# Two ring sizes in one weight stream: raw buffers from three to four, split buffers from six to five

## The chip, the cores and the metric

The kernel runs on one core of a Trainium2 chip. The metric is device time in microseconds of one execution. An execution was timed three times; the trace comes from one further, profiled execution. The engines of the core are named as the profile names them: PE is the matrix engine (TensorE), with PEld for its weight loads; DVE, ACT and POOL are the vector, scalar and GpSimd engines; SP is the engine that issues the weight loads.

## The reference, cut to what matters

Two transformer blocks run one after the other on 256 tokens of 1024 channels, batch 1, all in float32.

```python
# first block
mod = silu(c) @ ada_w + ada_b                    # six rows of 1024: shifts, scales, gates
u = rms_norm(h, norm1_g) * (1 + scale1) + shift1
z = u @ w_in                                     # q, k, v of two attentions, gates
y_a = nsa_attention(...) @ w_up_nsa              # 8 heads, softmax rows
y_b = stick_breaking_attention(...) @ w_up_sb
h = h + gate1 * ((sigmoid(m_a) * y_a + sigmoid(m_b) * y_b) @ w_out)
u2 = rms_norm(h, norm2_g) * (1 + scale2) + shift2
h = h + gate2 * (square(relu(u2 @ mlp_w1)) @ mlp_w2)
# second block
x = x + 0.5 * swiglu(rmsnorm(x, ffn1_norm), ffn1_w_gu, ffn1_w_down)
z = rmsnorm(x, mix_norm) @ w_in
merged = gate0 * (spatial_gating @ w_branch_a) + gate1 * (mla @ w_branch_b) + gate2 * (memory_attention @ w_branch_c)
x = x + merged @ w_out
x = x + 0.5 * swiglu(rmsnorm(x, ffn2_norm), ffn2_w_gu, ffn2_w_down)
```

The work is a long row of products of 256 tokens with weight matrices, and every weight is used once.

## The kernel before, in words

**The weight stream.** The host lays all weights out in the order of their use. The stream is cut into 191 chunks of up to 128 x 2048 float32 (1 MB), and each chunk into pieces of up to 1024 columns. Class `Stream` (L279) brings them in. `pump` (L303) issues the load of a chunk on SP (L320) into one of `RB` raw ring buffers of 8 KB a partition, once the chunk that had the buffer is used up. Some chunks of the start have buffers of their own and don't count.

**The split.** Each product is computed as three matmuls of numbers rounded to a short float: hi by hi, hi by lo, lo by hi. So each piece is split before use: `_split` (L332) writes hi on ACT (L342, tile wh), and lo, the difference of raw and hi, is written on DVE (L330, tile wl) when the next piece is split or the piece is used. hi and lo go into two pools of `HB` buffers each, of 4 KB a partition. A piece may only be split when fewer than `HB` pieces are split and not yet released (`_can`, L351); a piece is released by `done` behind its last product, and releases count in order.

**Which piece next.** After each product the program calls `fill` (L380), which splits up to three pieces as long as they lie at most four ahead of the one in use and `_can` allows it. So the place of a split in ACT's and DVE's order is set when the program is written: if `_can` says no, it is written after the next release, behind whatever other instructions the program has put on ACT and DVE in between. All engines work their instructions in order.

**What stands in the stream beside the split pieces.** The adaLN weights (labels `ada`) are not split: DVE multiplies them into a sum (L513; in the first normalization `first`, L506 and L509, with POOL taking some, L499). A finished sum is split itself for a column sum on PE: `put` (L356) takes a buffer of the hi and lo pools for it until `drop`. In the MLP this is so for gate2, from step p = 12 of the hidden columns to p = 14, where two copies (L1400) bring the row out.

**Where pieces are held long.** `lin_B` (L618) goes over its four pieces once for each half of the tokens and releases them in the second pass: this is so for the vb pieces of the attention stage and for the four kvm pieces of each half of the memory keys and values. `down_tail` (L1223) does the same with the last four pieces of a feed-forward stage, while it adds residuals (L1196, L1202) and takes squares for the next norm (L579, L581, L585).

**The attention stage.** Beside the products of the weight stream a planner interleaves the attention's own steps by estimated costs. `nsa` (L982) makes for each head a row block: scores on PE, the maximum on DVE (L995), exponentials on ACT (L997), the normalization on DVE (L999, L1000, L1002), then three transposes on PE (L1006) and a copy on ACT (L1008). Up to three heads go as a group; the tiles are ns2, ns3 and so on for the heads.

Of the kernel before, what the change touches and what calls it, by code (L numbers as in the profile page):

```python
# [276 lines left out]


class Stream:  # L279
    RB = 3  # L280
    HB = 6

    def __init__(self, tc, pools, wst, ada):
        self.nc, self.wst, self.ada = tc.nc, wst, ada
# [21 lines left out]
    def pump(self):  # L306
        while self.dma < len(CHUNKS):
# [3 lines left out]
            else:  # L311
                last = self.ring[-self.RB] if len(self.ring) >= self.RB else -1
                if last >= self._chunks_used():
# [37 lines left out]
    def _can(self):  # L351
        if self.at >= len(SUBS) or SUBS[self.at]["chunk"] >= self.dma:
            return False
        return SUBS[self.at]["kind"] == "ada" or self.seq - self.released < self.HB

    def put(self, t):  # L356

        assert self.seq - self.released < self.HB
        hi = self.hi_pool.tile([P, 1024], F32R, tag="whi", name=f"ph{self.seq}")
# [50 lines left out]
def _model(es, tc, nc, x_in, mem_in, wst, sm_in, rows_in, w1_in, cw2_in, sgw_in, posi_in, cst_in, cst1_in, oh_in, out, dbg):  # L410
# [3 lines left out]
    per = es.enter_context(tc.tile_pool(name="per", bufs=1))  # L414
    raw_p = es.enter_context(tc.tile_pool(name="raw", bufs=Stream.RB))
    hi_p = es.enter_context(tc.tile_pool(name="whi", bufs=Stream.HB))
    lo_p = es.enter_context(tc.tile_pool(name="wlo", bufs=Stream.HB))
    xp = es.enter_context(tc.tile_pool(name="xT", bufs=2))
# [1453 lines left out]
```

## Time and profile before

| what | value |
|---|---|
| three timed runs | 1081.32, 1081.81, 1083.03 us |
| median | 1081.81 us |
| profiled execution | 1083.37 us, its span 1081.6 us |
| busy: PE, PEld | 1047.4 us (97%), 946.7 us (88%) |
| busy: DVE, ACT, POOL | 689.3 us (64%), 573.8 us (53%), 77.5 us (7%) |
| weight stream's DMA queue | 198.74 MB, 50.7% of the DMA engines' time |
| 331 splits: hi on ACT, lo on DVE | 1029 ns and 1223 ns each |
| 1 MB load, issue to landing | 5.0 us (median of 170) |

PE is busy nearly all of the span, so idle time of the other engines costs nothing by itself. A row of the timeline gives start, duration, engine, line, operation, the tiles written and read, and in brackets how long the engine was idle before it and what ended the wait. PEclk in a row of windows is the granted clock of PE, 1.00 for the upper of two levels.

### The profile page before, as it was taken

The numbers are of one execution on the slowest core, as the hardware profiler recorded it, in microseconds if no ns is written. First come the engines' busy times: TensorE is split into PE (matmuls) and PEld (weight loads), VectorE is DVE, ScalarE is ACT, GpSimd is POOL, SyncE is SP. The second block draws the span as 40 slices with busy tenths as digits, with TensorE's granted clock in tenths as the row PEclk, the third lists the DMA queues.
The fourth block names the chain that finished last, engine by engine and source line by source line (L and its number), as shares of the span: only waits on it lengthen the run. The fifth ranks groups of instructions, "written<-read, shape, count | busy, mean of one in ns | idle before, by whom it ended". The sixth has DMA issues, their size and how long they took to land.

```text
span 1081.6 us, 16916 instructions
## 1 busy us (share of the span) xinstructions
PE 1047.4 (97%) x6909; PEld 946.7 (88%) x6909; DVE 689.3 (64%) x1058; ACT 573.8 (53%) x938; POOL 77.5 (7%) x85
## 2 busy tenths in 40 slices
PE   4899999999999999999999999999999999999998
PEld 3788678898899998889999998889999989999997
DVE  5976866768777665666545557578554886455543
ACT  5257565465664454555444445667666655444441
POOL 4400011120100010000000000100000500000000
PEclk9889999999999999999999999999999999999999
DMA  8675425755666645465555454744333655554541
GB/s 338 259 287 179 175 85 195 264 192 167 229 233 238 252 172 191 178 206 183 188 202 190 161 195 162 248 163 154 117 108 117 207 212 195 195 195 156 197 182 50
DMA packets 31961, 206.07 MB, mean 191 GB/s; under 512 B 3811, under 2 KB 5132, under 8 KB 9996
## 3 DMA queue, kind: packets, MB, share of 16 engines
q1 hardware_dynamic: 30028, 198.74, 50.7%
q0 software_dynamic: 1856, 6.26, 1.8%
q8 instruction: 54, 0.88, 0.3%
q14 instruction: 23, 0.19, 0.1%
HBM read 203.93 MB, written 1.06 MB: 190 GB/s over the span
## 4 chain that ended last, share of the span: by engine, by line
PE 77%; DVE 2%; ACT 1%; issue 0%; ACTq 0%
PE ps_a L455 39%; PE ps_w L455 36%; PE ps_t L561 1%; PE ps_t L455 1%; DVE wl L330 1%; PE ps_t L1718 0%; PE ps_w L1751 0%; PE ps_t L1790 0%; DVE u_l L611 0%; DVE xr L1196 0%; DVE SG L1195 0%; DVE SG L592 0%; PE ps_t L1574 0%; ACT x_h L602 0%; DVE SG L585 0%
## 5 line engine op out<-in xcount | busy, mean ns | idle before, releaser
L330 DVE TENSOR_TENSOR wl<-raw,wh 128x1024 fp32r<-128x1024 f32 (+2 forms) x331 | 392.6, 1223 | 76.9 <-ACT wh L342 76.4
L342 ACT ACTIVATE wh<-raw 128x1024 fp32r<-128x1024 f32 (+2 forms) x331 | 325.6, 1029 | 19.0 <-DMA raw<-in_wst_dram 9.9
L455 PE MATMUL ps_w<-x_h,wh 128*128 128x256 f32 x640 | 181.2, 283 | 0.0
L455 PE MATMUL ps_w<-x_h,wl 128*128 128x256 f32 x640 | 181.1, 283 | 0.0
L455 PE MATMUL ps_w<-x_l,wh 128*128 128x256 f32 x640 | 181.1, 283 | 0.0
L455 PEld LDWEIGHTS ps_w<-x_l,wh 128*128 128x128 f32 x640 | 122.7, 192 | 1.4
L455 PEld LDWEIGHTS ps_w<-x_h,wh 128*128 128x128 f32 x640 | 122.7, 192 | 1.4
L455 PEld LDWEIGHTS ps_w<-x_h,wl 128*128 128x128 f32 x640 | 122.7, 192 | 0.0
L455 PE MATMUL ps_w<-u_h,wh 128*128 128x256 f32 x224 | 63.4, 283 | 0.0
L455 PE MATMUL ps_w<-u_l,wh 128*128 128x256 f32 x224 | 63.4, 283 | 0.0
L455 PE MATMUL ps_w<-u_h,wl 128*128 128x256 f32 x224 | 63.4, 283 | 0.0
L455 PE MATMUL ps_a<-hmix_h,wh 128*128 128x256 f32 x192 | 57.1, 297 | 0.0
L455 PE MATMUL ps_a<-u_h,wh 128*128 128x256 f32 x192 | 56.5, 294 | 0.0
L455 PE MATMUL ps_a<-hmix_l,wh 128*128 128x256 f32 x192 | 54.3, 283 | 0.0
L455 PE MATMUL ps_a<-hmix_h,wl 128*128 128x256 f32 x192 | 54.2, 282 | 0.0
L455 PE MATMUL ps_a<-u_l,wh 128*128 128x256 f32 x192 | 54.2, 282 | 0.0
L455 PE MATMUL ps_a<-u_h,wl 128*128 128x256 f32 x192 | 54.2, 282 | 0.0
L455 PE MATMUL ps_a<-wh,hh 128*128 128x512 f32 x128 | 50.3, 393 | 0.0
L455 PE MATMUL ps_a<-wl,hh 128*128 128x512 f32 x128 | 50.1, 391 | 0.2 <-DVE wl L330 0.2
L455 PE MATMUL ps_a<-wh,hl 128*128 128x512 f32 x128 | 49.9, 390 | 0.0
L1420 ACT ACTIVATE f2r<-ps_w 128x256 f32<-128x256 f32 x20 | 7.7, 385 | 78.1 <-PE ps_w L455 78.1
L1421 DVE TENSOR_TENSOR f2r<-f2r,ps_w 128x256 f32<-128x256 f32 x20 | 8.4, 421 | 62.1 <-ACT f2r L1420 62.1
(494 smaller groups left out, 2400.7 us busy)
## 6 DMA issues: line engine op xcount, KB each, us to landing
raw<-in_wst_dram SPq DMA_DIRECT2D x170, 1024.0 KB, 5.0
raw<-in_wst_dram SPq DMA_DIRECT2D x9, 768.0 KB, 4.2
raw<-in_wst_dram SPq DMA_DIRECT2D x4, 792.0 KB, 8.2
raw<-in_wst_dram SPq DMA_DIRECT2D x3, 512.0 KB, 10.8
xr<-in_x_dram SPq DMA_DIRECT2D x2, 512.0 KB, 4.8
cw<-in_w_dram POOLq DMA_DIRECT2D x1, 1024.0 KB, 5.1
NB<-Dr SPq DMA_DIRECT2D x1, 1024.0 KB, 10.1
f<-in_rows_dram POOLq DMA_DIRECT2D x2, 512.0 KB, 4.3
```

The lines of the kernel that those rows point to most:

```text
L330: self.nc.vector.tensor_tensor(lo, raw, hi.bitcast(F32), op=OP.subtract)
L342: self.nc.scalar.activation(hi[:, :w], raw, AF.Copy)
L455: PE.matmul(o, l, r, start=start, stop=stop, skip_group_check=True)
L561: PE.transpose(bank[:, j * P:(j + 1) * P], src[:, (f0 + j) * P:(f0 + j + 1) * P], ident)
L1420: ACT.activation(r, b[:, :256], AF.Silu)
L1421: DVE.tensor_tensor(r, r, b[:, 256:512], op=OP.mult)
```

## The change

Two constants of `Stream`: the raw ring has four buffers of 8 KB a partition instead of three, and the hi and the lo pool have five buffers of 4 KB each instead of six. The bytes in SBUF stay the same.

```diff
 class Stream:
-    RB = 3
-    HB = 6
+    RB = 4
+    HB = 5
```

The pools are made with these sizes (`bufs=Stream.RB`, `bufs=Stream.HB`), and `pump`, `_can` and `put` decide by them. The orders of PE, POOL and SP stay as they were; on ACT and on DVE 18 splits stand later than before. Three of the places follow, with the numbers of pieces and chunks in the tiles' names (wl66 is the lo of piece 66, raw26 is chunk 26, ns2 is the block of head 2).

DVE's order in the attention stage before, from the products into the sum acc3 to the end of the second group of heads, the maxima and the first group left out:

```order
L513 SCALAR_TENSOR_TENSOR acc3_1080<-raw26_992,silu_c_104,acc3_1080 128x1024
L330 TENSOR_TENSOR wl66_1085<-raw26_992,wh66_1084 128x1024
...
L513 SCALAR_TENSOR_TENSOR acc3_1080<-raw27_1035,silu_c_104,acc3_1080 128x1024
L999 TENSOR_SCALAR nu1_1_1109<-nu1_1_1109 128x2
...
L1002 TENSOR_SCALAR ns1_1_1107<-ns1_1_1107,nu1_1_1109,GA_514 128x128
...
L1002 TENSOR_SCALAR ns2_1_1202<-ns2_1_1202,nu2_1_1204,GA_514 128x128
...
L1002 TENSOR_SCALAR ns3_1_1212<-ns3_1_1212,nu3_1_1214,GA_514 128x128
...
L330 TENSOR_TENSOR wl68_1252<-raw27_1035,wh68_1251 128x1024
...
L1002 TENSOR_SCALAR ns4_0_1222<-ns4_0_1222,nu4_0_1224,GA_514 128x128
...
L513 SCALAR_TENSOR_TENSOR acc3_1080<-raw28_1050,silu_c_104,acc3_1080 128x1024
```

DVE's order there now, from the same first product into acc3:

```order
L513 SCALAR_TENSOR_TENSOR acc3_1082<-raw26_900,silu_c_104,acc3_1082 128x1024
...
L999 TENSOR_SCALAR nu1_1_1105<-nu1_1_1105 128x2
...
L1002 TENSOR_SCALAR ns1_1_1103<-ns1_1_1103,nu1_1_1105,GA_516 128x128
...
L330 TENSOR_TENSOR wl66_1233<-raw26_900,wh66_1232 128x1024
...
L1002 TENSOR_SCALAR ns2_1_1197<-ns2_1_1197,nu2_1_1199,GA_516 128x128
...
L1002 TENSOR_SCALAR ns3_1_1207<-ns3_1_1207,nu3_1_1209,GA_516 128x128
...
L513 SCALAR_TENSOR_TENSOR acc3_1082<-raw27_994,silu_c_104,acc3_1082 128x1024
L330 TENSOR_TENSOR wl68_1254<-raw27_994,wh68_1253 128x1024
...
L1002 TENSOR_SCALAR ns4_0_1217<-ns4_0_1217,nu4_0_1219,GA_516 128x128
...
L513 SCALAR_TENSOR_TENSOR acc3_1082<-raw28_1037,silu_c_104,acc3_1082 128x1024
```

The lo of piece 66 stood ahead of the first group's maxima and now stands ahead of the second group's normalizations; the second product into acc3 stood ahead of the first group's normalizations and now stands between ns3 and ns4.

ACT's order in the MLP before, from the splits of chunk 79 (pieces 171 and 172, the latter m2 22) past the hidden row r14 and the two copies of gate2:

```order
L342 ACTIVATE wh171_3995<-raw79_3846 128x1024
L342 ACTIVATE wh172_3998<-raw79_3846 128x1024
L1338 ACTIVATE r14_4066<-ps_w1_22_4017 128x512
L1343 ACTIVATE hh14_4069<-r14_4066 128x512
L1400 ACTIVATE gate2_2636<-ps_w0_25_4073 128x512
L1400 ACTIVATE gate2_2636<-ps_w1_23_4077 128x512
L342 ACTIVATE wh173_4093<-raw80_3915 128x1024
L342 ACTIVATE wh174_4096<-raw80_3915 128x1024
```

ACT's order there now:

```order
L342 ACTIVATE wh171_3997<-raw79_3801 128x1024
L1338 ACTIVATE r14_4062<-ps_w1_22_4013 128x512
L1343 ACTIVATE hh14_4065<-r14_4062 128x512
L1400 ACTIVATE gate2_2638<-ps_w0_25_4069 128x512
L1400 ACTIVATE gate2_2638<-ps_w1_23_4073 128x512
L342 ACTIVATE wh172_4077<-raw79_3801 128x1024
L342 ACTIVATE wh173_4095<-raw80_3848 128x1024
L342 ACTIVATE wh174_4098<-raw80_3848 128x1024
```

The split of piece 172 went from ahead of the hidden row r14 to behind the copies of gate2.

DVE's order at the end of the MLP before, the lo of pieces 184 and 185 (the first two kvm pieces) and the residual rows of the first three quarters, with the gain of the next norm (L585):

```order
L330 TENSOR_TENSOR wl184_4272<-raw85_4158,wh184_4271 128x1024
L330 TENSOR_TENSOR wl185_4281<-raw86_4211,wh185_4280 128x1024
L1195 TENSOR_TENSOR rg0_4290<-ps_a0_14_2632,gate2_2636 128x512
L1196 TENSOR_TENSOR xr_97<-xr_97,rg0_4290 128x512
...
L1195 TENSOR_TENSOR rg0_4332<-ps_a2_11_2634,gate2_2636 128x512
L1196 TENSOR_TENSOR xr_97<-xr_97,rg0_4332 128x512
...
L585 TENSOR_TENSOR room1_2637<-xr_97,f1_2630 128x512
L330 TENSOR_TENSOR wl186_4349<-raw86_4211,wh186_4348 128x1024
```

DVE's order there now:

```order
L330 TENSOR_TENSOR wl184_4274<-raw85_4125,wh184_4273 128x1024
L1195 TENSOR_TENSOR rg0_4288<-ps_a0_14_2634,gate2_2638 128x512
L1196 TENSOR_TENSOR xr_97<-xr_97,rg0_4288 128x512
...
L1195 TENSOR_TENSOR rg0_4330<-ps_a2_11_2636,gate2_2638 128x512
L1196 TENSOR_TENSOR xr_97<-xr_97,rg0_4330 128x512
...
L585 TENSOR_TENSOR room1_2639<-xr_97,f1_2632 128x512
L330 TENSOR_TENSOR wl185_4344<-raw86_4160,wh185_4343 128x1024
L330 TENSOR_TENSOR wl186_4351<-raw86_4160,wh186_4350 128x1024
```

The lo of piece 185 went from ahead of the residual rows to behind the third quarter's gain, directly ahead of that of piece 186.

## Rows read from the trace of the kernel before

**Rows 1.** The page's head: busy time, share of the span, instructions, of each engine

```profile
PE 1047.4 (97%) x6909; PEld 946.7 (88%) x6909; DVE 689.3 (64%) x1058; ACT 573.8 (53%) x938; POOL 77.5 (7%) x85
```

**Rows 2.** Waits over the whole run: waiter, releaser, us in total, times, longest

```profile
ACT f2r L1420 <- PE ps_w L455: 78.1, 19, 4.4
...
ACT wh L342 <- DMA raw<-in_wst_dram: 9.9, 9, 2.6
```

**Rows 3.** Timeline of DVE, then of PE, in the first 60 us

```profile
12.82 4.29 DVE L509 SCALAR_TENSOR_TENSOR first<-raw,silu_c,first 128x512 f32<-128x512 f32 x3 [0.95 <-DMA raw<-in_wst_dram]
...
55.40 0.56 PE L455 MATMUL ps_t<-cst,first 128*128 128x1 f32 x2 [2.65 <-DVE first L509]
```

**Rows 4.** Timeline of DVE in the attention stage

```profile
117.00 1.22 DVE L330 TENSOR_TENSOR wl<-raw,wh 128x1024 fp32r<-128x1024 f32 x1
...
120.49 1.28 DVE L513 SCALAR_TENSOR_TENSOR acc<-raw,silu_c,acc 128x1024 f32<-128x1024 f32 x1
...
129.39 0.29 DVE L995 CUSTOM_DVE_ANT_0 ns<-ps_w,NB 128x128 f32<-128x128 f32 x1 [4.20 <-PE ps_w L455]
...
131.06 0.17 DVE L999 TENSOR_SCALAR nu<-nu 128x2 f32<-128x2 f32 x1
...
131.46 0.67 DVE L1002 TENSOR_SCALAR ns<-ns,nu,GA 128x128 f32<-128x128 f32 x2
...
133.51 1.23 DVE L330 TENSOR_TENSOR wl<-raw,wh 128x1024 fp32r<-128x1024 f32 x1 [0.40 <-ACT wh L342]
```

**Rows 5.** Timeline of ACT there, the second group's exponentials ending

```profile
132.34 0.19 ACT L997 ACTIVATION_READ_ACCUMULATOR ns<-ns,nm 128x1 f32 x1
132.44 1.04 ACT L342 ACTIVATE wh<-raw 128x1024 fp32r<-128x1024 f32 x1
```

**Rows 6.** Timeline of PE there, the transposes that wait, and the first ma matmul

```profile
108.99 0.76 PE L1006 MATMUL ps_w<-cst,ns 128*128 128x128 f32 x3 [2.10 <-DVE ns L1002]
...
123.94 0.76 PE L1006 MATMUL ps_w<-cst,ns 128*128 128x128 f32 x3 [0.69 <-DVE ns L1002]
124.92 0.76 PE L1006 MATMUL ps_t<-cst,ns 128*128 128x128 f32 x3 [0.23 <-DVE ns L1002]
...
135.46 0.76 PE L1006 MATMUL ps_t<-cst,ns 128*128 128x128 f32 x3 [0.49 <-DVE ns L1002]
135.97 0.37 PE L455 MATMUL ps_a<-u_h,wh 128*128 128x256 f32 x1
```

**Rows 7.** Windows: us, busy of PE, PEld, DVE, ACT, POOL, PEclk, DMA, GB/s

```profile
55.40:62.20 6.80, 6.80 (x24) 6.12 (x25) 3.75 (x10) 2.76 (x5) 0.00 (x0) 0.50 0.63 261
...
110.10:113.40 3.30, 3.30 (x12) 2.81 (x13) 3.23 (x7) 1.79 (x5) 0.00 (x0) 0.50 0.68 283
...
189.00:192.00 3.00, 2.11 (x16) 2.06 (x17) 2.84 (x4) 0.34 (x1) 0.84 (x1) 1.00 0.94 336
```

**Rows 8.** Timelines of ACT, DVE and PE in the MLP at gate2

```profile
424.00 5.79 ACT L342 ACTIVATE wh<-raw 128x1024 fp32r<-128x1024 f32 x6
...
425.09 5.77 DVE L330 TENSOR_TENSOR wl<-raw,wh 128x1024 fp32r<-128x1024 f32 x5 [1.23 <-ACT wh L342]
...
423.09 0.40 PE L455 MATMUL ps_a<-wh,hh 128*128 128x512 f32 x1
423.32 0.39 PE L455 MATMUL ps_a<-wl,hh 128*128 128x512 f32 x1
...
426.37 0.50 PE L455 MATMUL ps_a<-wl,hh 128*128 128x512 f32 x1 [0.16 <-DVE wl L330]
```

**Rows 9.** Timelines of ACT and PE at the first kvm pieces

```profile
457.14 3.89 ACT L342 ACTIVATE wh<-raw 128x1024 fp32r<-128x1024 f32 x4
...
458.18 0.39 PE L455 MATMUL ps_w<-wl,memT_h 128*128 128x512 f32 x1
```

**Rows 10.** Timelines of ACT and PE at the second half's kvm pieces

```profile
657.11 3.86 ACT L342 ACTIVATE wh<-raw 128x1024 fp32r<-128x1024 f32 x4
...
658.81 0.39 PE L455 MATMUL ps_w<-wl,memT_h 128*128 128x512 f32 x1
```

## The prediction

> **What bounds the kernel now.** I read the page's busy shares first: TensorE's matmuls fill 97% of the span [rows 1], so a change can only act through TensorE's idle time and its clock. Then the waits: summed over the run ACT waits 9.9 us, in nine pieces, for a weight load to land [rows 2], which is all that a shortage of raw buffers can show. Then the timeline of TensorE for its own gaps: those of 0.4 us or more after the first 24 us are eleven, 14.0 us in all by my count, at places with causes of their own: the adaLN sums of the start, the softmax rows ns of the attention stage (108.99, 123.94, 124.92), sbz, the hidden rows r of the MLP. The reader should see there that no gap repeats with the weight stream. So what decides is which of the split instructions the change puts behind other work, and whether TensorE then comes to them too early.
>
> **Part one, a fourth load.** SP issues the same 191 loads in the same order, each waiting for the ring buffer four loads back and not three; the orders of TensorE and POOL stay too. At the start the fifth ring load is issued some 7 us earlier, but loads land one after another, and DVE, which makes the adaLN sums, waits for a load for 0.95 us at 12.82 and not again in the next 40 us; TensorE's 2.65 us wait at 55.40 is for the DVE sum L509 [rows 3], and DVE has been busy with the sums and splits in order before it. So an earlier load shortens nothing there. Later, I followed each of ACT's nine waits for a load to the first matmul that uses its piece: none is followed by a TensorE wait for that piece. I take 0; the bounds are -1 (the 0.95 us of rows 3 handed through) and +1 (that same wait doubled, where one more load shares the DMA engines with those that DVE wants first).
>
> The Trainium skill (DMA: Bandwidth & Descriptors, Rules for kernel authors) says that a DMA is to be issued early and waited for late, so that its fixed cost overlaps. By it a fourth load would give back up to the 9.9 us of rows 2; the trace shows that these waits lie under TensorE's queue of ready pieces, so by the trace it gives none.
>
> **Part two, five pieces instead of six.** A piece's split is written into the program only when fewer than HB pieces are unreleased; where pieces are held long (the four vb pieces, the four last m2 pieces, the four kvm pieces, the column sum's own piece in the MLP), the next split now comes one release later, behind whatever the program writes in between. The order of ACT and DVE shows 18 splits that come later. I went through all 18: start from where ACT and DVE stand at the new place, add the split, compare with the first matmul on hi and on lo. Fourteen have 0.4 us or more to spare or cost 0.1 us together (the third query piece qm). Four are late.
>
> A split costs ACT 1.05 (1.04 at 132.44 in rows 5) and DVE 1.15 as a step, 1.23 to its end (133.51 in rows 4; neighbours on DVE overlap by some 0.08); an adaLN product costs DVE 1.20 (1.28 to its end, row 120.49 of rows 4). A normalization of one ns (L999, L1000, two of L1002) runs from 131.06 to 131.46 + 0.67 = 132.13 [rows 4], 1.07 alone and 1.0 in a row.
>
> First, the attention stage. wl66 leaves DVE's place at 117.00 and acc3's product the place at 120.49 [rows 4], ahead of the first ns group. That group gets up to 2.4 us of DVE; TensorE's waits of 0.69 and 0.23 at 123.94 and 124.92 [rows 6] go, so all is 0.92 earlier. Then ACT comes to wh66 behind the exponentials of the second group, which end at 132.34 + 0.19 = 132.53 [rows 5], now 131.61. wl66 stands on DVE ahead of ns2, which before had overlapped the exponentials. And acc3 stands between ns3 and ns4 beside wl68. From 131.61 the chain is wh66 1.05, wl66 1.15, ns2 1.0, ns3 1.0, acc3 1.20, wl68 1.15, ns4 1.07, and its transposes on TensorE 0.51 (135.46 + 0.51 reaches 135.97, rows 6): 8.13, so the first ma matmul starts at 139.74 and not at 135.97. Queued behind the waiting transposes are the ma and mb products, which wait for nothing else. Cost 3.8. No cover is left: TensorE has only the two other ns transposes in between. Below: 1.5, if the 2.4 us freed for the first group also brings the second group forward; above 4.7, if the early 0.92 is not gained.
>
> Second, m2 22 in the MLP. The column sum of gate2 holds a piece from step 12 to 14; with five the split of m2 22 waits for its release, behind the two gate2 copies on ACT, and starts where ACT now starts the next splits, at 424.00. hi is there at 425.06, lo, by the start of the first lo split at 425.09, at 425.09 + 1.23 = 426.32 [rows 8]. TensorE wants hi at 423.09 and lo one matmul (0.23) later. Its second matmul comes at 426.34 and not 423.32, but before it also lost time at the next piece: the second matmul there started at 426.37 [rows 8]; now it starts twelve matmuls of 0.23 (423.09 to 423.32) after 426.34, at 429.1. Cost 2.7. The row bounds it tightly; what could go is 0.3 either way.
>
> Third, the second kvm piece. Its split falls behind the square of the residual on ACT and starts at 457.14; lo is ready at 457.14 + 1.05 + 1.25 = 459.44, TensorE wants it at 458.18 [rows 9]. Cost 1.3. Fourth, the same piece of the other kvm half: ACT at 657.11, lo at 659.42, wanted at 658.81 [rows 10]. Cost 0.6. Both could be 0 if the split gets ahead, and neither over 2.3, a whole split on both engines.
>
> Stalls: 3.8 + 2.7 + 1.3 + 0.6 + 0.1 = 8.5 us. Bounds by the terms: 1.5 + 2.4 = 3.9 and 4.7 + 3.0 + 2.3 + 2.3 = 12.3.
>
> **The clock.** After TensorE's wait of 2.10 us [rows 6] its granted clock stands at the half level, 1.2 of 2.4 GHz, for 3.3 us, and after that of 2.65 us for 6.8 us; after the wait of 1.39 us at 189.89 it stays at 1.00 [rows 7]. A stretch of 3.3 us at half level while TensorE is busy throughout costs 1.7. In the attention stage the wait before ns4 is about 2.9, longer than any of these: one stretch, 1.7. At m2 22 there is a wait of 2.0, a matmul, and 0.8 more: between the row that brought it and the one that didn't, nearer to the first, but broken in two; I take half of a stretch, 0.85. From both sides: 0, and 5.1 (one stretch of 3.3 us and one of 6.8).
>
> **Sum.** 8.5 + 2.5 = 11.0 us. The profiled run took 1083.37 us (span 1081.6 and 1.8 around it), so its counterpart would take 1094.4. It lies 1.56 above the median of the runs shown, 1081.81, and from that the forecast is 1092.8 us.
>
> **Rivals.** First, smaller: the attention term mostly vanishes because the second group comes forward with the first, and the clock stays. For it: DVE gets 2.4 us back ahead of the first group. Against: between the two groups DVE idles for 4.20 us until TensorE has made the scores [rows 4], so DVE's lead does not pass on. Time 1081.8 + 1.5 + 4.7 = 1088.0.
>
> Second, no change at all, the moved splits being in time or the pieces being released earlier than the trace has it: 1081.8. Against it stand the four rows above, each of which ends after TensorE's own.
>
> Third, faster: the earlier loads take the start's waits. For it, TensorE's wait of 2.65 us at 55.40 and the half level behind it for 6.8 us [rows 3, 7], which together are 2.65 + 3.4 = 6.1; with part two costing little, 1081.8 - 6.1 + 2 = 1077.7. Against it: DVE shows no wait for a load there.
>
> Fourth, much slower, one mechanism: in both feed-forward stages of the second block the third split after each hidden row must wait for TensorE to release the fifth piece back, up to 2.4 us by my count, and the delay reaches TensorE. It decides only where ACT's slack behind it is below that; ACT then waits up to 4.4 us for the next hidden product, 78.1 us in 19 waits in the last stage alone [rows 2]. At 0.5 us in each of 38 groups, 19 to a stage, it would be 1092.8 + 19 = 1111.8.
>
> The Trainium skill (Perfetto Trace Analysis, Optimization Strategy) says that one gap that repeats on the engine that should be saturated can mean too few buffers for the next tile; the fourth rival is where this would be seen. The trace of before has no such gap with six, and the 4.4 us of slack speak against one with five.
>
> **How the numbers follow.** The forecast with its clock term 45%, the same stalls without it (1090.3) 28%, the smaller case 12%, much slower 4%, no change 7%, faster 4%. The range 1086.5 to 1096.5 holds the first three; its ends are a little under the smaller case and the forecast with 3.7 more, toward the 5.1 bound of the clock and the upper stalls. What a measurement here can't tell from no change is 0.2%, 2.2 us: faster by more than that 4%, within it 7%, slower 89%.
>
> **What would show it.** TensorE gaps near 133 to 139 us for ns on DVE, near 424 us for wh and wl of m2, near 459 and 660 us for wl; ACT's waits for loads fewer than nine, with nothing gained by it; the granted clock at one half after the first of these gaps. The forecast is wrong if TensorE does not wait for wl at 424 us, if the start up to 62 us runs shorter by over 1 us, or if TensorE shows a repeated gap for wl in the feed-forward stages.

## The result, and the profile after

The changed kernel takes 1094.9 us (median of four runs, 1093.32 to 1095.32), the kernel before, on the same chips, 1082.42; the ratio is 1.0108 with a 95% interval of 1.0085 to 1.0132. The profiled execution took 1093.32 us with a span of 1091.6, 10.0 more than the span before.

The head of the page after, in the form of [rows 1], and below it the waits of ACT and DVE over the whole run, in the form of [rows 2]:

```profile
PE 1051.9 (96%) x6909; PEld 949.1 (87%) x6909; DVE 693.0 (63%) x1058; ACT 583.9 (53%) x938; POOL 78.7 (7%) x85
```

```profile
DVE wl L330 <- ACT wh L342: 110.7, 117, 3.1
...
ACT wh L342 <- PE ps_w L455: 78.1, 55, 1.8
...
ACT f2r L1420 <- PE ps_w L455: 35.4, 19, 1.9
...
ACT wh L342 <- PE ps_a L455: 32.9, 33, 2.6
...
ACT wh L342 <- DMA raw<-in_wst_dram: 0.5, 1, 0.5
```

Both halves of the change did what they say. ACT's waits for a load went from 9.9 us in nine pieces [rows 2] to 0.5 us in one. In their place ACT waits 111 us, 88 times, for TensorE to release a split buffer, where it waited 8.4 us, 11 times, before. Nearly all of this is idle time that ACT had anyway: its waits for the next hidden products went from 78.1 us [rows 2] to 35.4 for f2r, and from 70.4 to 33.8 for f1r, the same step of the second block's first feed-forward stage. So the largest new row of the waits is not where the time went.

To find it, I paired the 6909 matmuls of the two traces, whose order is the same, and followed how much later each starts after the change: 2.3 us earlier at 62 us and still at 121 us, 0.75 later at the waiting ns4 transposes, 3.0 later at 141 us, the same up to 420 us (3.2), 6.2 later at the second matmul of m2 22, 8.5 at 440 us, 9.9 from 468 us to the end. The attention stage, m2 22 in the MLP and one kvm piece make up all of the loss; the 2.3 us of lead at the start are another matter, treated below.

TensorE's timeline in the attention stage after, in the columns of [rows 6]:

```profile
131.91 0.76 PE L1006 MATMUL ps_w<-cst,ns 128*128 128x128 f32 x3 [1.14 <-DVE ns L1002]
132.90 0.76 PE L1006 MATMUL ps_w<-cst,ns 128*128 128x128 f32 x3 [0.22 <-DVE ns L1002]
136.21 1.01 PE L1006 MATMUL ps_t<-cst,ns 128*128 128x128 f32 x3 [2.55 <-DVE ns L1002]
136.87 0.56 PE L455 MATMUL ps_a<-u_h,wh 128*128 128x256 f32 x1
```

DVE's timeline there, with the lo of piece 66, the acc3 product and the lo of piece 68 ahead of the normalizations, to be held against [rows 4]:

```profile
129.97 1.23 DVE L330 TENSOR_TENSOR wl<-raw,wh 128x1024 fp32r<-128x1024 f32 x1 [2.37 <-ACT wh L342]
131.11 0.16 DVE L999 TENSOR_SCALAR nu<-nu 128x2 f32<-128x2 f32 x1
...
133.08 1.28 DVE L513 SCALAR_TENSOR_TENSOR acc<-raw,silu_c,acc 128x1024 f32<-128x1024 f32 x1
134.27 1.22 DVE L330 TENSOR_TENSOR wl<-raw,wh 128x1024 fp32r<-128x1024 f32 x1
135.41 0.16 DVE L999 TENSOR_SCALAR nu<-nu 128x2 f32<-128x2 f32 x1
```

DVE idles 2.37 us for the hi of piece 66, which ACT makes behind the exponentials, while the exponentials of all three heads come ready to be normalized, the last at 128.99. TensorE waits at each of the three transposes, the last time behind acc3 and the lo of piece 68.

ACT and TensorE at m2 22, then TensorE at the second kvm piece, in the columns of [rows 8, 9]:

```profile
427.15 4.83 ACT L342 ACTIVATE wh<-raw 128x1024 fp32r<-128x1024 f32 x5
...
428.26 0.74 PE L455 MATMUL ps_a<-wh,hh 128*128 128x512 f32 x1 [1.85 <-ACT wh L342]
429.52 0.80 PE L455 MATMUL ps_a<-wl,hh 128*128 128x512 f32 x1 [0.52 <-DVE wl L330]
...
468.00 0.50 PE L455 MATMUL ps_w<-wl,memT_h 128*128 128x512 f32 x1 [0.77 <-DVE wl L330]
```

The splits start behind the gate2 copies, and TensorE waits for the hi and then for the lo of the same piece. The granted clock behind both places, in the columns of [rows 7]:

```profile
125.00:131.00 6.00, 5.77 (x30) 4.32 (x30) 2.79 (x13) 4.76 (x15) 0.00 (x0) 1.00 0.00 0
...
136.80:143.50 6.70, 6.70 (x38) 5.56 (x37) 2.65 (x3) 2.41 (x4) 2.34 (x1) 0.64 0.81 303
143.50:150.00 6.50, 6.50 (x44) 5.18 (x42) 4.96 (x26) 4.25 (x16) 0.41 (x1) 1.00 0.00 1
...
430.00:434.60 4.60, 4.60 (x12) 3.55 (x12) 4.01 (x4) 1.99 (x3) 0.00 (x0) 0.50 0.92 315
434.70:440.00 5.30, 5.30 (x33) 4.71 (x33) 2.43 (x2) 2.04 (x2) 0.00 (x0) 0.96 0.83 301
```

At each place the clock is at the lower level, wholly or in part, while TensorE is busy throughout: 0.64 on the mean of 6.7 us, and 0.50 for 4.6 us. In whole, waits included, it stands at 0.50 from 134.8 to 141.6 us and from 428.3 to 435.1 us. Neither stretch is there before: the same stages, from 136 to 143 and from 424 to 429 us, have 1.00 throughout:

```profile
136.00:143.00 7.00, 7.00 (x49) 5.39 (x48) 4.41 (x12) 5.43 (x15) 2.76 (x2) 1.00 0.83 293
424.00:429.00 5.00, 4.84 (x21) 3.67 (x20) 3.91 (x4) 5.00 (x7) 0.00 (x0) 1.00 0.15 23
```

### The profile page after: what moved, and what is told of

The parts are those of the page before. It is cut to its first block, busy times and chain, and to the rows that moved or that the text cites. A ratio compares the mean times of both kernels' runs of the same rounds, so it can differ in the third digit from the quotient of the medians.

```text
span 1091.6 us, 16942 instructions
## 1 busy us (share of the span) xinstructions
PE 1051.9 (96%) x6909; PEld 949.1 (87%) x6909; DVE 693.0 (63%) x1058; ACT 583.9 (53%) x938; POOL 78.7 (7%) x85
## 4 chain that ended last, share of the span: by engine, by line
PE 58%; ACT 1%; DVE 1%; issue 0%; ACTq 0%
PE ps_a L455 29%; PE ps_w L455 27%; PE ps_t L561 1%; ACT wh L342 0%; PE ps_t L1718 0%; PE ps_t L455 0%; DVE wl L330 0%; PE ps_w L1751 0%; PE ps_t L1790 0%; DVE xr L1196 0%; DVE rg L1195 0%; ACT junk L579 0%; ACT QL L1629 0%; ACT L555 0%; ACT x_h L602 0%
## 5 line engine op out<-in xcount | busy, mean ns | idle before, releaser
L330 DVE TENSOR_TENSOR wl<-raw,wh 128x1024 fp32r<-128x1024 f32 (+2 forms) x331 | 396.8, 1225 | 113.7 <-ACT wh L342 110.7
L342 ACT ACTIVATE wh<-raw 128x1024 fp32r<-128x1024 f32 (+2 forms) x331 | 336.7, 1033 | 133.2 <-PE ps_w L455 78.1
L455 PEld LDWEIGHTS ps_w<-u_h,wh 128*128 128x128 f32 x224 | 42.9, 192 | 0.5
L455 PEld LDWEIGHTS ps_w<-u_l,wh 128*128 128x128 f32 x224 | 42.9, 192 | 0.5
## 6 DMA issues: line engine op xcount, KB each, us to landing
raw<-in_wst_dram SPq DMA_DIRECT2D x3, 512.0 KB, 14.3
```

The source lines that it names most:

```text
L330: self.nc.vector.tensor_tensor(lo, raw, hi.bitcast(F32), op=OP.subtract)
L342: self.nc.scalar.activation(hi[:, :w], raw, AF.Copy)
L455: PE.matmul(o, l, r, start=start, stop=stop, skip_group_check=True)
```

## The experiments

The theory after the result: the loss is the splits that the program writes later, at the places above, and the half clock behind two of them; the fourth raw buffer does nothing. Rivals: the fourth load itself gains (the lead of 2.3 us at 62 us) or costs; the clock falls anyway; taken away at one place, the wait comes up at another.

### The second half of the change alone (three raw buffers, five split buffers)

Against the kernel before:

```diff
     RB = 3
-    HB = 6
+    HB = 5
```

> Three raw buffers and five split buffers: the second half of the change alone. Theory: the whole cost comes from the splits that are written later, so this takes what the full change takes, 1093 to 1096 us, with waits of the matrix engine near 133 to 136, 428 and 468 us (the places of the full change, shifted by under 3 us). Rival one, the fourth load gains: the full change's trace is 2.3 us ahead of the old one at 62 us; if the load does that, this run shows no such lead and takes about 2.3 us more, 1097. Rival two, the fourth load costs (one more load shares the DMA engines): about 1084 to 1088.

Measured 1095.7 us (1095.27 to 1096.13), ratio to the kernel before 1.0112 (1.0096 to 1.0128), against 1.0108 with four raw buffers. The waits are those of the full change (1.14 and 2.55 us near 134 and 138, 1.85 and 0.76 near 431, 0.76 at 471). So the cost is the split buffers'; the rival that the fourth load costs falls. ACT waits for loads 3.6 us here and 0.5 us with the fourth buffer, and that buys nothing that can be measured; by the two intervals, a gain or a loss of up to some 3 us can't be excluded. Four raw and six split buffers, the first half of the change alone, were not run, so all of this is shown at five split buffers only.

The lead at the start isn't the load's either. Against the one trace of before, the traces of kernels with four raw buffers are at 62.5 us 2.3 us ahead, 0.1 behind, 0.2 ahead, 0.2 ahead, 0.1 behind and 2.1 ahead, in the order in which they are told here, and this one, with three, is 1.2 ahead. At 66 us, when the last stretch at half clock of the start is over in all of them, the six lie between 2.3 us ahead and 1.1 behind, 0.4 ahead on the mean, and this one is 0.6 ahead. The instructions of the start have the same order in all; the waits for the sums L509 and the half clock behind them fall out differently from run to run.

### The column sum one step earlier

Against the full change:

```diff
-        if p == 14:
+        if p == 13:
             for h in range(2):
                 b = column_sum(parts, h)
```

> The full change with gate2's column sum one step earlier (p = 13 instead of 14), so that its piece is released before m2 22 is split. Theory: the waits of 1.85 and 0.52 us near 428 us go, and with them the stretch at half clock behind them: 2.7 + 2.7 us less, about 1089.5. Rival: the half level behind the waits is not their doing and comes anyway, 2.7 us less, about 1092.

Measured 1090.07 us (1088.07 to 1090.32), ratio 1.0055 (1.004 to 1.007): by the medians 4.8 us less than the full change, by the ratios 5.7. TensorE's timeline at the column sum's new place, and windows over it and over m2 22 (which starts near 429 here):

```profile
417.31 0.50 PE L455 MATMUL ps_w<-ph,onesr 128*128 128x512 f32 x1 [0.95 <-DVE r L1339]
```

```profile
417.30:421.00 3.70, 3.69 (x16) 3.09 (x17) 1.82 (x2) 3.63 (x6) 0.00 (x0) 1.00 0.73 301
...
429.00:433.00 4.00, 4.00 (x21) 3.31 (x20) 2.39 (x3) 2.96 (x4) 0.00 (x0) 1.00 0.27 113
```

The wait of 0.95 us for r moved along with the sum, as it was before the change too (1.01). The two waits at m2 22 are gone, and with them the half level: TensorE is busy for the whole 4 us at 1.00. So the clock's fall at this place is the doing of TensorE's waits there. Which of them is not shown: the wait of 1.01 us for r, which stood ahead of the other two at 425.68, left the place with the sum; in the old kernel it brought no fall by itself.

At the attention stage, which this edit leaves as the full change has it, TensorE has the same wait of 2.55 us before ns4 (at 140.20), but here the half level lasts for a shorter time behind it, 3.4 us, and costs 1.05 us instead of 2.15:

```profile
139.80:143.20 3.40, 3.00 (x14) 2.86 (x15) 3.00 (x4) 1.44 (x2) 0.36 (x1) 0.50 0.77 251
143.20:149.00 5.80, 5.80 (x38) 4.19 (x38) 2.36 (x10) 3.50 (x11) 2.39 (x2) 1.00 0.60 219
```

### The vb stage's later splits behind the attention's steps

In the second pass over the vb pieces the planner's step comes first, and the splits only behind the last piece. The edit is to `lin_B` of the full change, with a parameter `late` (its lines are left out here) that is set for the vb pieces alone.

```diff
+                if late and t == 1:
+                    tick(3 * len(ks_of[s]) * width / 2400)
+                    if s == len(labels) - 1:
+                        S.fill()
+                    continue
                 S.fill()
```

> The full change with the splits in the second pass over the vb pieces written behind the attention's own steps, so that the lo of piece 66, the acc3 product and the lo of piece 68 stand behind all three normalizations of the second group. Theory: the waits of 1.14, 0.22 and 2.55 us near 132 to 136 us go, 3.0 us net, and the stretch at half clock behind them, 2.0 us: about 1090. Rival: the piece mb 0 is now itself late, since its split stands behind the group's last copies, and the wait only moves to it: 1093 to 1095.

Measured 1095.6 us (1092.6 to 1096.15), ratio 1.0104 (1.0087 to 1.0121): nothing gained. The three waits for ns are gone, and the first ma matmul comes 2.3 us ahead of before, but by 145 us TensorE is late again. Its timeline, then DVE's, POOL's and ACT's, and the clock behind:

```profile
142.09 2.07 PE L455 MATMUL ps_a<-PCT,VBD 120*128 120x256 f32 x4 [3.60 <-DVE ot_l L567]
...
136.86 1.28 DVE L513 SCALAR_TENSOR_TENSOR acc<-raw,silu_c,acc 128x1024 f32<-128x1024 f32 x1
138.05 3.38 DVE L330 TENSOR_TENSOR wl<-raw,wh 128x1024 fp32r<-128x1024 f32 x1
141.35 0.68 DVE L567 TENSOR_TENSOR ot_l<-ps_a,ot_h 128x512 fp32r<-128x512 f32 x1
...
137.66 2.68 POOL L362 TENSOR_TENSOR pl<-acc,ph 128x1024 fp32r<-128x1024 f32 x1 [17.39 <-ACT ph L361]
...
134.60 2.02 ACT L342 ACTIVATE wh<-raw 128x1024 fp32r<-128x1024 f32 x2
```

```profile
142.00:149.00 7.00, 6.91 (x20) 4.72 (x21) 3.25 (x20) 2.85 (x12) 0.41 (x1) 0.50 0.43 150
```

The rival was right that the wait only moves, but wrong about where: not mb 0 is late but ot_l, the lo of the attention's output, which stands on DVE behind the three moved instructions, one of them held by POOL (the last section). That lo took 3.38 us instead of 1.22, so without it the wait of 3.60 us would be some 1.4 us (an estimate from these rows). With the wait the clock falls to the half level from 140.6 to 150.7 us.

### Both edits

The two diffs above, together.

> The full change with both edits, the column sum one step earlier and the later splits in the second pass over vb. Theory: only the kvm piece's 1.3 us are left of the cost, so 1083 to 1085 with no gain at the start, 1081 to 1083 if the lead of 2.3 us at the start is the fourth load's. Rival: other moved splits, hidden behind these waits until now, come up instead: over 1087.

Measured 1089.76 us (1087.83 to 1090.59), ratio 1.0055 (1.0039 to 1.007), the same as the column sum alone. The rival holds: the attention's wait for ot_l is there again, 3.60 us at 142.38.

### Only acc3 and the lo of piece 68 behind ns4

```diff
-                S.fill()
+                if not (late and (t, s) == (1, 2)):
+                    S.fill()
```

> The full change without the split that is written behind the third of the four vb pieces in the second pass: on DVE only the acc3 product and the lo of piece 68 move, from between ns3 and ns4 to behind ns4; the lo of piece 66 stays ahead of ns2. Theory: the wait of 1.14 us for ns2 stays, the one of 2.55 us for ns4 goes; what stands behind it on DVE (ot_l) gets up to 1 us later, with POOL's lo of the column sum's piece near it, so 1.5 to 2.4 us less, and 2.0 less for the half clock: 1090.5 to 1092. Rival: as in the run with all splits moved, the wait only goes on to the next thing that DVE makes, ot_l, and is as long there: 1094 to 1096.

The edit is again to `lin_B` of the full change, for the vb pieces alone. Measured 1090.94 us (1090.3 to 1092.02), ratio 1.008 (1.0068 to 1.0093): by the medians 4.0 us less than the full change, by the ratios 3.0. TensorE's timeline at the three transposes, DVE's with the two moved instructions and ot_l, and the clock behind:

```profile
135.96 0.76 PE L1007 MATMUL ps_w<-cst,ns 128*128 128x128 f32 x3 [1.14 <-DVE ns L1003]
136.94 0.76 PE L1007 MATMUL ps_w<-cst,ns 128*128 128x128 f32 x3 [0.22 <-DVE ns L1003]
137.92 0.76 PE L1007 MATMUL ps_t<-cst,ns 128*128 128x128 f32 x3 [0.22 <-DVE ns L1003]
...
138.11 1.28 DVE L513 SCALAR_TENSOR_TENSOR acc<-raw,silu_c,acc 128x1024 f32<-128x1024 f32 x1
139.31 1.22 DVE L330 TENSOR_TENSOR wl<-raw,wh 128x1024 fp32r<-128x1024 f32 x1
142.28 0.69 DVE L567 TENSOR_TENSOR ot_l<-ps_a,ot_h 128x512 fp32r<-128x512 f32 x1 [1.76 <-ACT ot_h L566]
```

```profile
136.00:142.00 6.00, 5.56 (x35) 3.99 (x36) 4.38 (x11) 3.16 (x6) 1.69 (x1) 1.00 0.69 199
```

The wait before ns4 falls from 2.55 to 0.22 us, the one before ns2 stays at 1.14, and the clock stays at 1.00. Here the moved work is done while DVE would idle for ot_h.

At m2 22, which this edit leaves alone, TensorE's waits are nearly those of the full change (1.85 us at 428.06 and 0.77 at 429.32), but the stretch at half level is half as long, 3.4 us, and the place costs 4.3 us in all instead of 5.35:

```profile
430.00:433.40 3.40, 3.40 (x10) 2.62 (x9) 3.40 (x4) 1.79 (x2) 0.00 (x0) 0.50 0.94 316
433.40:440.00 6.60, 6.60 (x45) 6.10 (x45) 2.86 (x3) 2.91 (x3) 0.00 (x0) 1.00 0.86 331
```

### That edit and the column sum

> That edit and the column sum one step earlier, together. Theory: the two savings add up, 4.8 us from the column sum as measured alone and what the other edit gives: 1085.5 to 1087. Rival: the attention edit gives nothing, 1090.

Measured 1085.51 us (1082.58 to 1086.33), ratio 1.0021 (1.001 to 1.0032): the savings add up. What is left, 0.2%, is by the pairs of matmuls mainly the wait for ns2 (1.14 us, against the 0.69 and 0.23 us of [rows 6] that it saves earlier; 0.8 us net) and the kvm piece (0.77 us at 458.15, and a late hi ahead of it; 1.4 us).

### Two raw buffers

Against the kernel before:

```diff
-    RB = 3
+    RB = 2
     HB = 6
```

> Two raw buffers, six split buffers: the first half of the change in the other direction; ACT's, PE's, POOL's and SP's orders are those of the old kernel. Theory: the raw ring is not short, so two buffers cost little: ACT waits more often for loads, but TensorE has four pieces ready ahead of it: 1082 to 1087. Rival: loads bound the stream as soon as the ring is tight (a load takes 5.0 us to land, a chunk lasts 5.7 us on TensorE): over 1095.

Measured 1111.08 us (1110.18 to 1111.82), ratio 1.0267 (1.0253 to 1.0281). My theory was wrong and the rival right. The waits, then ACT and TensorE near 360 us:

```profile
ACT wh L342 <- DMA raw<-in_wst_dram: 145.6, 62, 6.9
```

```profile
354.92 1.06 ACT L342 ACTIVATE wh<-raw 128x1024 fp32r<-128x1024 f32 x1 [5.85 <-DMA raw<-in_wst_dram]
...
360.37 0.39 PE L455 MATMUL ps_w<-u_h,wl 128*128 128x256 f32 x1 [2.62 <-DVE wl L330]
```

A load is issued only when the chunk two back is split, so nearly its whole landing time comes between two splits: the load that ACT waits for until 354.92 was issued at 350.19, as the lo ended that freed its buffer (350.16). The pieces ahead of TensorE run out: by the pairs of matmuls, 10.6 of this trace's 26.8 us are lost in the MLP (300 to 440 us of the old kernel's time) and 8.0 from there to 480 us. From two to three raw buffers is worth 28.6 us by the medians (with six split buffers), from three to four nothing that can be measured (with five).

### Two raw buffers and seven split buffers

Against the kernel before:

```diff
-    RB = 3
-    HB = 6
+    RB = 2
+    HB = 7
```

> Two raw buffers and seven split buffers: the exchange of the change in the other direction. Theory: one more piece can be split ahead where pieces are held, so the old kernel's waits for ns near 124 and 135 us and for lo near 426 us shrink, 1 to 2 us less than with two and six: 1081 to 1086. Rival: with six no split is late any more, so seven give nothing and the time is that of two and six.

Measured 1119.55 us (1118.03 to 1122.02), ratio 1.0345 (1.0329 to 1.0361). My theory was wrong, and so was the rival: seven split buffers take 8.5 us more than six, far outside the intervals. By the pairs of matmuls the two traces are even at 870 us (26.8 us behind the old kernel with six, 26.9 with seven); then seven loses 11.7 us between 907 and 937 us, at the norm ahead of the last feed-forward stage, where six loses nothing. ACT and TensorE at the longest of the waits there:

```profile
930.02 1.06 ACT L342 ACTIVATE wh<-raw 128x1024 fp32r<-128x1024 f32 x1 [4.47 <-DMA raw<-in_wst_dram]
...
932.67 1.08 ACT L602 ACTIVATE x_h<-ps_t 128x512 fp32r<-128x512 f32 x2
...
933.31 0.80 PE L455 MATMUL ps_w<-wh,x_h 128*128 128x512 f32 x1 [4.91 <-ACT x_h L602]
```

With seven this split is written ahead of the second half of the norm's output x_h, with six behind it. ACT waits 4.47 us for the split's load, and x_h stands behind it. So a deeper pool can cost too, by a split that is written too early and whose load has not landed. Three and six, the old kernel's, is the best of the five pairs tried.

## Why the prediction was right

The forecast was 1092.8 us in 1086.5 to 1096.5, slower by four late splits and two stretches of half clock; 1094.9 was measured. The mechanism was right at three of the four splits and at both stretches; that the sum came as near is in part luck, since two stall terms were 0.6 us too large each and the two clock terms together 2.3 us too small. By its steps, from the traces:

- **The fourth load: 0, measured not apart from 0.** ACT's waits for loads went and TensorE gained nothing; with five split buffers the ratio is 1.0108 with it and 1.0112 without. The profiled run's lead of 2.3 us at the start is the spread of the start, which the bounds of 1 us around this term left out. The forecast set itself the mark that over 1 us at the start would make it wrong; the mark was too tight for a single trace, since kernels with the same start spread over 3.4 us by 66 us.
- **The attention stage: 3.8, measured 3.2** (the shift goes from -2.3 to 0.9 us at the first ma matmul). The chain runs as written: exponentials, wh66, wl66, ns2, ns3, acc3, wl68, ns4. The early gain was 1.2 us (the matmul at 125.44 before starts 3.6 us earlier, from 2.4 ahead of it), not 0.92, and the chain a little shorter.
- **m2 22: 2.7, measured 2.7** (3.0 from 3.2 to 6.2, less the old wait at the next piece).
- **The kvm pieces: 1.3 and 0.6, measured 1.4 and 0.** The step that failed: I set ACT's new split at its old time, 657.11 [rows 10], and asked only what stands behind it. But the removed lo also frees DVE ahead of the residual rows, whose squares ACT waits for; ACT came there 8.95 us later than before while TensorE was 9.9 later, and the lo was in time. I had counted such a gain in the attention stage, and not here.
- **The clock: 1.7 and 0.85, measured 2.2 and 2.6** (from 0.90 to 3.05 us of shift, and 5.35 of m2 22's whole loss less the 2.7). The step that failed is the half stretch at m2 22: two waits of 1.85 and 0.52 us with one matmul between brought a full stretch, and it lasted past the 3.3 us of [rows 7]. But how long a stretch lasts is not fixed by the waits: behind the same ones as here it lasted 3.4 us and not 6.8 in the attention stage of the run with the column sum moved (1.05 us lost), and at m2 22 of the run with only acc3 and the lo of piece 68 moved (1.6 us beyond the 2.7). Nor does a wait's length alone decide whether one comes: behind the 2.62 us at 360.37 with two raw buffers the clock stays at 1.00 (360.4 to 367.0). The forecast's choice between waits of 1.39 and 2.10 us found that a stretch would come; its size is chance.
- **The sum.** The terms are 3.2 + 2.7 + 1.4 + 4.8 = 12.1 us, where 11.0 was forecast, less the 2.3 us of this trace's start: 9.8 of the 9.9 us between the two traces. The ratio of the timed runs, 1.08%, of 1082.4 is 11.7 us (9.2 to 14.3 by its interval), near the 12.1 that the terms give without the start's chance.
- **The rivals.** The much slower one has its mechanism in the trace, ACT waiting for a buffer's release 88 times; f2r's wait, 35.4 us still left of 78.1, shows the slack that hides it. The smaller one, the second ns group coming forward, didn't happen: DVE waited 4.22 us for its scores, as before (4.20, [rows 4]).
- **A reading.** Of TensorE's eleven gaps of 0.4 us or more before, which the forecast names by place, 124.92 is not one (0.23 us); 135.46 is (0.49 us). The sum of 14.0 us is right, and nothing rests on the place.

## What to carry to other kernels

When the depth of a ring changes, don't ask how deep it is but what its `_can` lets the program write where: on engines that work in order, one release later can mean behind a whole group of foreign instructions, and each such split is priced by the time its engine reaches the new place against the first matmul that uses it. Count what a moved instruction frees at its old place with the same care as what it delays at the new one. A deeper pool moves splits as well, and can bring one ahead of other work while its load is still under way. And a wait that ends on the busiest engine can be paid twice, if its clock falls behind it: in the changed kernel's trace 5.9 us of waiting at two places cost 4.8 more. Price that part as a range: in other traces nearly the same waits cost 1.1 us less at either place.

## What the runs showed of the hardware that was not expected

- A DVE subtraction of 128 x 1024 with its usual time of 1.22 us took 3.38 us at 138.05 in the run with all vb splits moved, while POOL's subtraction of the same size ran from 137.66 to 140.34; it ended 1.09 us after POOL's did. The kernel before has such a place too, in the MLP:

```profile
402.57 3.28 DVE L330 TENSOR_TENSOR wl<-raw,wh 128x1024 fp32r<-128x1024 f32 x1
...
401.68 3.09 POOL L362 TENSOR_TENSOR pl<-acc,ph 128x1024 fp32r<-128x1024 f32 x1 [117.49 <-ACT ph L361]
```

  There DVE's ended 1.08 us after POOL's. So where POOL's had begun first, DVE's waited for nearly all of it; where DVE's had begun first (139.31 in the run with only acc3 and the lo of piece 68 moved), it took its 1.22 us. The Trainium skill (Perfetto Trace Analysis, Optimizing Scalar/DVE Operations) says that GpSimd and DVE share a read port of SBUF, so that moving work between them may not help; these traces agree, with a price of 2.2 and 2.1 us for the two overlaps.
- One and the same order of instructions at the start spreads over 3.4 us by 66 us between profiled executions of six kernels with four raw buffers, through waits of 0.5 to 3.0 us for the adaLN sums and the clock behind them.
- Two raw buffers cost 28.6 us although a load lands in 5.0 us and a chunk lasts 1081.6 / 191 = 5.7 us on TensorE on the mean. The rows at 350 to 360 us show a load issued only when its buffer is free and then waited for; that this comes of splits in bunches, which the mean hides, is my reading and was not tested.
